# One interruption per query tile or chunk, earlier chunk loads, and all weight remainders on VectorE, in a hybrid attention and Mamba-2 block

## The chip, the cores and the metric

The kernel runs on one core of a Trainium2 chip. It is one decoder block on 512 tokens, in one launch. The metric is device time in microseconds (us). Five engines work side by side, each through its own instructions in their order, and wait for each other by semaphores: TensorE (PE in the profile, its weight loads PEld), VectorE (DVE), ScalarE (ACT), GpSimd (POOL), and SyncE (SP), which here issues all DMA transfers.

## The reference, cut to what matters

```python
h = rms_norm(x, norm_mix_g)                               # x: 512 tokens x 1024
q, k, v, z, xbc, dt_raw, gate_logits = split(h @ w_in)    # 1024 -> 10272 columns
# attention branch: 8 heads, two maps of 64 per head, values of 128
q = rms_norm(q) * scale; k = rms_norm(k)
for i in range(4):                                        # query tiles of 128
    logits = einsum('hmqd,hmkd->hmqk', q[tile i], k) + t5_bias, causal
    p = softmax(logits);  a = p[:, 0] - lam * p[:, 1]
    o[tile i] = a @ v
y_attn = rms_norm(o, attn_subln_g) * (1 - lam_init)
# Mamba-2 branch: 4 groups of 8 heads, state of 128
xbc = silu(causal_dwconv(xbc)); xs, bm, cm = split(xbc); dt = softplus(dt_raw + dt_bias)
for c in range(4):                                        # chunks of 128 tokens
    cum = cumsum(dt * a); decay = exp(cum[:, None] - cum[None, :]), causal
    y_diag = ((cc @ bc.T) * decay) @ xc
    y_off = (cc @ state) * exp(cum)
    state = state * exp(total) + (bc * w).T @ xc
y = rms_norm((y + xs * d_skip) * silu(z))                 # by group
mixed = sigmoid(g_attn) * (y_attn @ w_proj_attn) + sigmoid(g_ssm) * (y_ssm @ w_proj_ssm)
x = x + mixed @ w_out
u = causal_dwconv(rms_norm(x) @ w_up)
x = x + (silu(u_gate) * u_val) @ w_down                   # 2816 hidden columns
```

## The kernel before, in words

**Weights.** All weights stand in one stream `ws` of units of 128x1024 floats, in the order in which they are used (179 units, list `order` at the end of the file). `Weights.load` (L76) brings the next unit: a DMA writes `wr` (L80), ScalarE rounds it to the faster format as `wh` (L82), and a subtraction makes the remainder `wl` (L85). It runs on VectorE, but for units 71 to 90 on GpSimd (`pool_units`, L74 and L84). Every large product is three matmuls of 512 columns: `wh` by the rounded activations, `wh` by their remainder, `wl` by the rounded ones (L201 to L203 and like lines). Here these are called projections.

**The state-space stage.** 64 projection units (`SSD_UNITS`) run one after the other: B, C, x and z tiles of a group, the gate tiles e, and p, the products of a finished group with `w_proj_ssm`. After unit n the program adds what the dictionary `at` holds under n; these are the small steps, in full-precision matmuls that interrupt the projections. `SSD_AT` (L59) gives per group the units after which they stand. `chunk_pre` (L377) loads the decay rows of a chunk (`dec`), makes their exponentials on ScalarE, and the product of C and B (L388) times `dec` on VectorE (L391). `chunk_state` (L404) is the product with the state (L412, tile `yo`) and the new state (L419). `chunk_out` (L429) is the diagonal part (L435), which reads `dec`. `chunk_stat` (L445) sums squares, and `group_norm` (L459, L466 to L471) makes `yH` and `yL`, which the p units read. Tokens of x and B are turned by `flip` (L305, L308). The steps take their PSUM tiles from the pool `sm` (3 buffers).

**The attention stage.** `pieces` is a list of pieces of projections of about 6 to 12 matmuls: `pair_pieces` make q, k and v of two heads, `gate_pieces` a gate tile, `pa_pieces` three of the tiles of `w_proj_attn`. The dictionary `todo` holds what stands behind each piece. For a head, `prep` (L585) transposes q and k into two buffers (L591, pool `tpp`, 2 buffers), and ScalarE and VectorE read them (L599 to L607; `ql` is L601). Then come, for each of four query tiles, `logits` (L616), `flip_a` (L649, also from `tpp`) and `values` (L657); the last `values` of a head starts a chain over ScalarE, VectorE (`rsqrt`, L113) and GpSimd (L677), and `head_out` (L679, L682, again from `tpp`) needs its end. In the last pair the chain's end is what the rest of the kernel (from L756) waits for.

**What sets the order.** The program's order and the pools are given; a scheduler of the framework lays out the queues of the five engines from it, and may put an instruction a few places later or earlier where it reckons with a wait. Each engine then takes its queue strictly in order.

Of the kernel before, what the change touches and what calls it, by code (L numbers as in the profile page):

```python
# [9 lines left out]
F32 = mybir.dt.float32  # L10
# [8 lines left out]
P = 128  # L19
S = 512  # L20
D = 1024
NK = 8
NCH = 4
NG = 4
HPG = 8
NH = 8
# [18 lines left out]
def _units():  # L45
# [6 lines left out]
    for g in (2, 3):  # L52
# [3 lines left out]


SSD_UNITS = _units()
SSD_AT = [(11, (12, 14, 16, 18), (12, 15, 17, 19), 21, 23),  # L59
# [3 lines left out]


class Weights:


    def __init__(self, tc, ctx, ws, ahead):
        self.nc, self.tc, self.ws, self.ahead = tc.nc, tc, ws, ahead
        self.raw = ctx.enter_context(tc.tile_pool(name="wraw", bufs=3))  # L70
        self.parts = ctx.enter_context(tc.tile_pool(name="wparts", bufs=4))
        self.at = 0
        self.ready = []
        self.pool_units = frozenset(range(71, 91))  # L74

    def load(self, ahead=None):  # L76
        nc = self.nc
        with self.tc.high_priority(offset=ahead or self.ahead):
            raw = self.raw.tile([P, 1024], F32, name="wr")
            nc.sync.dma_start(out=raw, in_=self.ws[self.at])  # L80
            hi = self.parts.tile([P, 1024], F32R, name="wh")
            nc.scalar.copy(out=hi, in_=raw)  # L82
            lo = self.parts.tile([P, 1024], F32R, name="wl")
            eng = nc.gpsimd if self.at in self.pool_units else nc.vector  # L84
            eng.tensor_sub(out=lo, in0=raw, in1=hi.bitcast(F32))  # L85
        self.at += 1
        self.ready.append((hi, lo))

# [7 lines left out]
def block_kernel(ctx, tc, xt, ws, cols, heads, lams, relb, ident_d, ut_d, onehot_d, mline_d, out):  # L96
    nc = tc.nc
# [115 lines left out]
    cum_d = dram.tile([NG, NCH, HPG, P], F32, name="cum_d")  # L213
    ecum_d = dram.tile([32, S], F32, name="ecum_d")
# [75 lines left out]
    groups = [{} for _ in range(NG)]  # L290
# [20 lines left out]
    def tokens_b(st):  # L311
        tp = flip(st["B"])
        st["Bt"] = sp.tile([P, NCH, P], F32, name="Bt")
        A.copy(out=st["Bt"].rearrange("p c n -> p (c n)"), in_=tp)
# [10 lines left out]
    def unit(n, name, g):  # L325
        kind, j = name[0], int(name[1]) if len(name) > 1 else 0
        st = groups[g]
        if kind == "B":
            st["B"] = sp.tile([P, S], F32, name="Bc")
            conv_tile(16 + g, st["B"])  # L330
            at.setdefault(n + (2 if n else 4), []).append(lambda: tokens_b(st))
        elif kind == "C":
            st["C"] = sp.tile([P, S], F32, name="Cc")
            conv_tile(20 + g, st["C"])
        elif kind == "x":
            if j == 0:
                st["x"] = [sp.tile([P, S], F32, name="xtok", bufs=8) for _ in range(NCH)]
                st["Y"] = sp.tile([P, 4, S], F32, name="Y")
            xc = sp.tile([P, S], F32, name="xc", bufs=3)
            conv_tile(4 * g + j, xc)  # L340
            A.activation(out=st["Y"][:, j], in_=xc, func=AF.Copy, scale=pc[:, C_DK + 4 * g + j:C_DK + 4 * g + j + 1])
            at.setdefault(n + (3 if n < 4 else 2), []).append(lambda: tokens_x(g, j, xc))
        elif kind == "z":
            if j == 0:
                st["z"] = sp.tile([P, 4, S], F32, name="sz")
            ps = in_ctile()
            zs = st["z"][:, j]
            V.scalar_tensor_tensor(out=zs, in0=ps, scalar=0.5, in1=r_bc, op0=ALU.mult, op1=ALU.mult)
            zt = sp.tile([P, S], F32, name="raw")
            A.activation(out=zt, in_=zs, func=AF.Tanh)  # L350
            V.scalar_tensor_tensor(out=zs, in0=zt, scalar=1.0, in1=zs, op0=ALU.add, op1=ALU.mult)
        elif kind == "e":
            if j % 4 == 0:
                gates.append(sp.tile([P, 4, S], F32, name="Y" if j else "sz"))
            ps = in_ctile()
            gt = gates[-1][:, j % 4]
            V.tensor_mul(out=gt, in0=ps, in1=r_bc)
            A.activation(out=gt, in_=gt, func=AF.Tanh, scale=0.5)
        else:
            h, l = W.next()  # L360
            for i in range(2):
                c = 2 * j + i
                ps = ctile(lambda k: (h[:, (i * 4 + k) * P:(i * 4 + k + 1) * P], l[:, (i * 4 + k) * P:(i * 4 + k + 1) * P]),
                           4, lambda k: st["yH"][:, k, :], lambda k: st["yL"][:, k, :])
                if g == 0:
                    A.copy(out=acc[c], in_=ps)
                else:
                    V.tensor_add(out=acc[c], in0=acc[c], in1=ps)
                if g == NG - 1:
                    V.scalar_tensor_tensor(out=acc[c], in0=gates[c // 4][:, c % 4], scalar=1.0, in1=acc[c],  # L370
                                           op0=ALU.add, op1=ALU.mult)
# [2 lines left out]
    h3 = lambda t: t.rearrange("p (h d) -> p h d", h=HPG)  # L374
    j4 = lambda t: t.rearrange("p (j l) -> p j l", j=4)

    def chunk_pre(g, c):  # L377

        st = groups[g]
        cs = slice(c * P, (c + 1) * P)  # L380
        dec = sp.tile([P, HPG, P], F32, name="dec", bufs=3)
        nc.sync.dma_start(out=dec, in_=cum_d[g, c].partition_broadcast(P))
        for h in range(HPG):
            A.activation(out=dec[:, h], in_=dec[:, h], func=AF.Relu, scale=-1.0,
                         bias=qcol[:, 0, c, g * HPG + h:g * HPG + h + 1])
        A.activation(out=dec, in_=dec, func=AF.Exp, scale=-1.0)
        pcb = sm.tile([P, S], F32, name="sm")[:, :P]
        T.matmul(pcb, lhsT=st["B"][:, cs], rhs=st["C"][:, cs], start=True, stop=True)  # L388
        cb = sp.tile([P, P], F32, name="cb")
        V.tensor_mul(out=cb, in0=pcb, in1=ut)  # L390
        V.tensor_mul(out=dec, in0=dec, in1=cb.unsqueeze(1).to_broadcast([P, HPG, P]))  # L391
        st["dec", c] = dec
        if c < NCH - 1:
            xw = st["xw", c] = sp.tile([P, S], F32, name="xw")
            G.tensor_mul(out=h3(xw), in0=h3(st["x"][c]),
                         in1=qcol[:, 1, c, g * HPG:(g + 1) * HPG].unsqueeze(2).to_broadcast([P, HPG, 64]))
        if c > 0:
            ec = st["ec", c] = sp.tile([P, 4, P], F32, name="ec")
            for m in range(2):
                nc.sync.dma_start(out=ec[m * 64:(m + 1) * 64], in_=bass.AP(  # L400
                    tensor=ecum_d.tensor, offset=ecum_d.offset + (g * HPG + m) * S + c * P,
                    ap=[[0, 64], [2 * S, 4], [1, P]]))

    def chunk_state(g, c):  # L404

# [64 lines left out]
            A.copy(out=st["yH"][:, j], in_=Y[:, j])  # L470
            V.tensor_sub(out=st["yL"][:, j], in0=Y[:, j], in1=st["yH"][:, j].bitcast(F32))  # L471

    for g, (first, states, outs, last, norm) in enumerate(SSD_AT):
        def put(n, f, *a):
            at.setdefault(n, []).append(lambda: f(*a))
        put(first, chunk_pre, g, 0)
        for c in range(NCH):
            put(states[c], chunk_state, g, c)
            if c > 0:
                put(outs[c], chunk_stat, g, c - 1)  # L480
            put(outs[c], chunk_out, g, c)
            if c + 1 < NCH:
                put(outs[c], chunk_pre, g, c + 1)
        put(last, chunk_stat, g, NCH - 1)
        put(norm, group_norm, g)

# [225 lines left out]
    for p_ in range(4):  # L712
        start.append(len(pieces))
        if p_ < 3:
            pieces += pair_pieces(p_ + 1) + gate_pieces(p_)
        else:
            for c in range(3, 8):
                pieces += gate_pieces(c)
            pa = [pa_pieces(c) for c in range(3)]
            pieces += [f for q in pa for f in q[:3]] + [q[3] for q in pa]  # L720
# [1 line left out]
    def put(n, f, *a):  # L722
        todo.setdefault(n, []).append(lambda: f(*a))

    put(start[0] - 3, prep, 0)
    for p_ in range(4):
        for e, (prep_at, ats) in enumerate(zip((5, 22), ((0, 3, 7, 10), (14, 17, 21, 24)) if p_ < 3 else ((0, 3, 6, 9), (12, 15, 18, 21)))):
            h = 2 * p_ + e
            if h < NH - 1:
                put(start[p_] + prep_at, prep, h + 1)  # L730
            for i, n in enumerate(ats):
                n += start[p_]
                lag = 7 if p_ < 3 else 6
                put(n, logits, h, i)
                put(n + lag, flip_a, h, i)
                put(n + lag + 2, values, h, i)
            put(ats[3] + start[p_] + lag + 7, head_out, h)
    for n, f in enumerate(pieces):
        f()
        for g in todo.pop(n, []):  # L740
# [188 lines left out]
```

## Time and profile before

| | |
|---|---|
| median of three runs | 1175.27 us (1171.23 to 1176.12) |
| the profiled execution | 1176.51 us |
| its span, first to last instruction | 1174.7 us |
| mean granted TensorE clock | 0.984 |
| busy: TensorE matmul, VectorE, ScalarE, GpSimd | 1130.8, 770.5, 579.2, 166.5 us |
| state-space units | about 48 to 410 us of the span |
| q, k, v of the first two heads | about 410 to 475 us |
| attention, heads among projections | about 475 to 737 us |
| w_proj_attn, w_out, and the gated MLP | from about 737 us |

The matmul spans overlap, since matmuls are pipelined, so a busy TensorE can still lose time: what counts is how far apart two starts lie, and the waits. A wait is shown with the instruction that ended it. A stretch's granted clock (PEclk) is 1.00 at 2.4 GHz and 0.50 at 1.2 GHz. Durations of VectorE instructions include time in which the engine stood still inside them.

### The profile page before, as it was taken

What the parts mean: (1) busy time and instruction counts of PE and PEld (TensorE: products, weight loads), DVE (VectorE), ACT (ScalarE), POOL (GpSimd) and SP (SyncE); (2) the same over time, 40 slices, a digit from 0 to 9 for tenths busy, and PEclk for the clock granted to TensorE, in tenths of its full rate; (3) what the DMA queues carried; (4) which work ended last, traced back from release to release, by engine and by line L of the source; (5) the groups of instructions that cost most, each with busy time, mean ns of one, the idle gap of its engine ahead of it and who ended that gap; (6) DMA issues with size and microseconds to landing.
All of it is one profiled execution on the core that took longest, in us unless ns stands there. A gap on an engine that the chain in (4) does not pass through costs nothing.

```text
span 1174.7 us, 15747 instructions
## 1 busy us (share of the span) xinstructions
PE 1130.8 (96%) x5934; PEld 956.2 (81%) x5934; DVE 770.5 (66%) x1259; ACT 579.2 (49%) x1122; POOL 166.5 (14%) x177
## 2 busy tenths in 40 slices
PE   7999998999999999998989997999999999999998
PEld 5788876887887889998888876887888888888887
DVE  7858777768786573576767874745777777772221
ACT  5785655765664233656556663334444444441120
POOL 1003212112132201432432100012000000000000
PEclk9999998999999999998989999999999999999999
DMA  7463332333432222221212120343233332333420
GB/s 243 114 125 112 112 110 88 112 116 114 125 112 95 83 90 85 74 76 59 78 59 69 62 73 18 109 160 108 90 92 106 90 102 95 93 105 108 120 96 18
DMA packets 56124, 114.46 MB, mean 97 GB/s; under 512 B 20640, under 2 KB 28496, under 8 KB 56048
## 3 DMA queue, kind: packets, MB, share of 16 engines
q1 hardware_dynamic: 56048, 113.45, 31.6%
q8 instruction: 47, 0.77, 0.3%
q14 instruction: 29, 0.24, 0.1%
HBM read 111.19 MB, written 2.24 MB: 97 GB/s over the span
## 4 chain that ended last, share of the span: by engine, by line
PE 87%; DVE 7%; ACT 3%; issue 2%; POOL 1%; DMA 0%; SPq 0%; ACTq 0%; POOLq 0%; DVEq 0%
PE mm L201 20%; PE mm L202 20%; PE mm L203 20%; PE mm L524 4%; PE mm L522 4%; PE mm L523 4%; PE po L663 1%; DVE wl L85 1%; PE sm L435 1%; PE mm L539 1%; PE mm L540 1%; PE mm L538 1%; PE mm L756 1%; PE mm L757 1%; PE mm L758 1%
## 5 line engine op out<-in xcount | busy, mean ns | idle before, releaser
L82 ACT CAST wh<-wr 128x1024 fp32r<-128x1024 f32 x179 | 187.4, 1048 | 229.8 <-PE mm L202 190.5
L85 DVE TENSOR_TENSOR wl<-wr,wh 128x1024 fp32r<-128x1024 f32 x159 | 196.7, 1238 | 106.7 <-ACT wh L82 105.1
L201 PE MATMUL mm<-xH,wh 128*128 128x512 f32 x392 | 159.2, 406 | 7.8 <-ACT xH L173 7.2
L202 PE MATMUL mm<-xL,wh 128*128 128x512 f32 x392 | 154.9, 395 | 0.0
L203 PE MATMUL mm<-xH,wl 128*128 128x512 f32 x392 | 154.7, 395 | 0.0
L201 PE MATMUL mm<-hH,wh 128*128 128x512 f32 x352 | 137.1, 390 | 0.0
L203 PE MATMUL mm<-hH,wl 128*128 128x512 f32 x352 | 137.0, 389 | 0.0
L202 PE MATMUL mm<-hL,wh 128*128 128x512 f32 x352 | 137.0, 389 | 0.0
L522 PE MATMUL mm<-wh,xH 128*128 128x256 f32 x384 | 111.3, 290 | 0.0
L524 PE MATMUL mm<-wh,xL 128*128 128x256 f32 x384 | 109.9, 286 | 0.0
L523 PE MATMUL mm<-wl,xH 128*128 128x256 f32 x384 | 109.7, 286 | 0.0
L201 PEld LDWEIGHTS mm<-xH,wh 128*128 128x128 f32 x392 | 74.6, 190 | 24.1 <-ACT xH L173 7.2
L202 PEld LDWEIGHTS mm<-xL,wh 128*128 128x128 f32 x392 | 74.6, 190 | 16.0 <-DVE xL L174 1.0
L203 PEld LDWEIGHTS mm<-xH,wl 128*128 128x128 f32 x392 | 74.4, 190 | 16.3 <-DVE wl L85 0.3
L202 PEld LDWEIGHTS mm<-hL,wh 128*128 128x128 f32 x352 | 66.1, 188 | 13.8
L201 PEld LDWEIGHTS mm<-hH,wh 128*128 128x128 f32 x352 | 66.1, 188 | 13.7
L203 PEld LDWEIGHTS mm<-hH,wl 128*128 128x128 f32 x352 | 66.1, 188 | 13.5
L523 PEld LDWEIGHTS mm<-wl,xH 128*128 128x128 f32 x384 | 74.4, 194 | 0.3
L524 PEld LDWEIGHTS mm<-wh,xL 128*128 128x128 f32 x384 | 74.4, 194 | 0.0
L522 PEld LDWEIGHTS mm<-wh,xH 128*128 128x128 f32 x384 | 74.2, 193 | 0.2
L201 PE MATMUL mm<-aH,wh 128*128 128x512 f32 x176 | 68.5, 389 | 0.0
L202 PE MATMUL mm<-aL,wh 128*128 128x512 f32 x176 | 68.5, 389 | 0.0
(240 smaller groups left out, 2264.9 us busy)
## 6 DMA issues: line engine op xcount, KB each, us to landing
wr<-in_ws SPq DMA_DIRECT2D x179, 512.0 KB, 3.5
dec<-cum_d SPq DMA_DIRECT2D x16, 512.0 KB, 5.2
ec<-ecum_d SPq DMA_DIRECT2D x24, 128.0 KB, 3.9
x<-in_xt SPq DMA_DIRECT2D x4, 512.0 KB, 4.7
xr<-in_xt SPq DMA_DIRECT2D x8, 256.0 KB, 2.6
out_y<-x SPq DMA_DIRECT2D x8, 256.0 KB, 2.0
b<-line_d SPq DMA_DIRECT2D x8, 128.0 KB, 2.8
pc<-in_cols SPq DMA_DIRECT2D x1, 173.5 KB, 3.7
```

The lines of the kernel that those rows point to most:

```text
L82: nc.scalar.copy(out=hi, in_=raw)
L85: eng.tensor_sub(out=lo, in0=raw, in1=hi.bitcast(F32))
L201: T.matmul(ps, lhsT=h, rhs=rH(k), start=(k == 0), stop=False)
L202: T.matmul(ps, lhsT=h, rhs=rL(k), start=False, stop=False)
L203: T.matmul(ps, lhsT=l, rhs=rH(k), start=False, stop=(k == n - 1))
L435: T.matmul(yd[(h % 2) * 64:(h % 2) * 64 + 64, (h // 2) * P:(h // 2 + 1) * P], lhsT=xk[:, h * 64:(h + 1) * 64], rhs=dec[:, h], start=True, ...
L522: T.matmul(ps, lhsT=xH[k][:, sl], rhs=h, start=(k == 0), stop=False)
L523: T.matmul(ps, lhsT=xH[k][:, sl], rhs=l, start=False, stop=False)
L524: T.matmul(ps, lhsT=xL[k][:, sl], rhs=h, start=False, stop=(k == NK - 1))
L538: T.matmul(ps, lhsT=hk, rhs=xH[k], start=(k == 0), stop=False)
L539: T.matmul(ps, lhsT=hk, rhs=xL[k], start=False, stop=False)
L540: T.matmul(ps, lhsT=lk, rhs=xH[k], start=False, stop=(k == NK - 1))
```

## The change: what it does

Three things are changed. In the state-space stage a chunk has one place instead of two: the state part, the diagonal part, the preparation of the next chunk and the old chunk's sum all stand after one unit, with the token flips in front of them. The loads of `dec` and `ec` become a step of their own (`chunk_load`), two chunks ahead, and the first preparation of a group stands 3 or 4 units before its first chunk. The norm of group 0 stands after unit 22 instead of 23.

In the attention stage 37 steps are laid over the pieces. At step n stand the logits of query tile n, the flip of tile n-2 and the values of tile n-3. `prep` moves to 5 or 6 pieces before a head's first step, `head_out` to two steps behind the head's last values. Gate tile 2 moves from the third stretch of pieces to the last.

All remainders are subtracted on VectorE; `pool_units` goes.

```diff
-SSD_AT = [(11, (12, 14, 16, 18), (12, 15, 17, 19), 21, 23),
+SSD_AT = [(8, 10, (12, 14, 16, 19), 21, 22),
...
-        self.pool_units = frozenset(range(71, 91))
...
-            eng = nc.gpsimd if self.at in self.pool_units else nc.vector
-            eng.tensor_sub(out=lo, in0=raw, in1=hi.bitcast(F32))
+            nc.vector.tensor_sub(out=lo, in0=raw, in1=hi.bitcast(F32))
...
-            at.setdefault(n + (3 if n < 4 else 2), []).append(lambda: tokens_x(g, j, xc))
+            at.setdefault(n + (3 if n < 4 else 2), []).insert(0, lambda: tokens_x(g, j, xc))
...
+    def chunk_load(g, c):
+        st = groups[g]
+        dec = st["dec", c] = sp.tile([P, HPG, P], F32, name="dec", bufs=3)
+        nc.sync.dma_start(out=dec, in_=cum_d[g, c].partition_broadcast(P))
+        if c > 0:
+            ec = st["ec", c] = sp.tile([P, 4, P], F32, name="ec")
...
-    for g, (first, states, outs, last, norm) in enumerate(SSD_AT):
+    for g, (dec0, xw0, chunks, last, norm) in enumerate(SSD_AT):
         def put(n, f, *a):
             at.setdefault(n, []).append(lambda: f(*a))
-        put(first, chunk_pre, g, 0)
-        for c in range(NCH):
-            put(states[c], chunk_state, g, c)
+        put(dec0 - 1, chunk_load, g, 0)
+        put(dec0, chunk_pre, g, 0)
+        put(xw0, chunk_load, g, 1)
+        put(xw0, chunk_in, g, 0)
+        for c, n in enumerate(chunks):
             if c > 0:
-                put(outs[c], chunk_stat, g, c - 1)
-            put(outs[c], chunk_out, g, c)
+                put(n, chunk_stat, g, c - 1)
+            put(n, chunk_state, g, c)
+            put(n, chunk_out, g, c)
+            if c + 2 < NCH:
+                put(n, chunk_load, g, c + 2)
             if c + 1 < NCH:
-                put(outs[c], chunk_pre, g, c + 1)
+                put(n, chunk_pre, g, c + 1)
+                put(n, chunk_in, g, c + 1)
...
-    put(start[0] - 3, prep, 0)
+    steps = []
     for p_ in range(4):
-        for e, (prep_at, ats) in enumerate(zip((5, 22), ((0, 3, 7, 10), (14, 17, 21, 24)) if p_ < 3 else ((0, 3, 6, 9), (12, 15, 18, 21)))):
...
+        steps += [start[p_] + n for n in ((0, 3, 7, 10, 14, 17, 21, 24) if p_ < 2 else range(0, 24, 3))]
+    steps += [steps[-1] + n for n in (3, 6, 9, 12, 15)]
+    for h in range(NH):
+        first = steps[4 * h] if h else start[0] + 1
+        put(first - 6 if h % 2 else first - 5, prep, h)
+    for n in range(4 * NH + 5):
+        for f, back in ((logits, 0), (flip_a, 2), (values, 3)):
+            if 0 <= n - back < 4 * NH:
+                put(steps[n], f, (n - back) // 4, (n - back) % 4)
+        if n >= 8 and n % 4 == 0:
+            put(steps[n], head_out, n // 4 - 2)
```

Three places in the queues show it. In the changed file a line stands 2 lines higher up to L375, and up to 11 lines lower behind that. The first is TensorE's queue where group 0 is normed (`tp<-t,ones`) and the first chunk of group 1 runs. Before:

```order
L466 MATMUL tp<-t_1496,ones 128x128 x4
L419 MATMUL sm<-xw,Bt 128x512
L435 MATMUL sm<-dec,xtok 64x128 x8
L388 MATMUL sm<-Cc,Bc 128x128
L412 MATMUL sm<-Cc,state 128x128 x4
L201 MATMUL mm<-yH,wh 128x512 x2
```

The same place in the changed kernel:

```order
L306 MATMUL mm<-ident,Bc 128x128 x4
L471 MATMUL tp<-t_1519,ones 128x128 x2
L424 MATMUL sm<-xw,Bt 128x512
L471 MATMUL tp<-t_1519,ones 128x128 x2
L440 MATMUL sm<-dec,xtok 64x128 x8
L396 MATMUL sm<-Cc,Bc 128x128
L199 MATMUL mm<-xH_87,wh 128x512
```

Before, the product that reads `yH` follows at once, with the second chunk's state part (L412) pulled ahead of it; now a z tile of 24 projections stands in between, and the second chunk's part comes after the p and x units.

The second is VectorE's queue around the `prep` of head 2, whose `ql` frees a transpose buffer. Before:

```order
L643 RECIPROCAL es<-sums 128x2
L645 SCALAR_TENSOR_TENSOR cf<-es,nlam,sums 128x1
L646 SCALAR_TENSOR_TENSOR p<-p,cf 128x384
L601 TENSOR_TENSOR ql_3907<-tp,qq_4962 64x512
L633 TENSOR_TENSOR lg<-lg,bias 128x256
L601 TENSOR_TENSOR ql_3908<-tp,qq_4966 64x512
```

The same place in the changed kernel:

```order
L657 SCALAR_TENSOR_TENSOR p<-p,cf 128x384
L83 TENSOR_TENSOR wl<-wr,wh 128x1024 x2
L644 TENSOR_TENSOR lg<-lg,bias 128x256
L684 TENSOR_SCALAR ov<-ov 128x4
L644 TENSOR_TENSOR lg<-lg,bias 128x256
L115 TENSOR_SCALAR rsi<-ov 128x4
L612 TENSOR_TENSOR ql_3907<-tp,qq_4975 64x512
L116 TENSOR_SCALAR rsy<-rsi 128x4
L618 SCALAR_TENSOR_TENSOR ks_4983<-tp,gqk,ks_4983 64x512
L118 SCALAR_TENSOR_TENSOR rst<-rsy 128x4
```

Two subtractions that stood on GpSimd now stand ahead of `ql`, and `ql` stands among the small instructions of the head's `rsqrt`.

The third is TensorE's queue at the end of the last head. Before:

```order
L663 MATMUL po<-vt,aT 128x128 x4
L701 MATMUL mm<-yaH_3883,wh 128x512
L702 MATMUL mm<-yaL_3891,wh 128x512
L703 MATMUL mm<-yaH_3883,wl 128x512
...
L682 MATMUL tp<-ident,o 128x128 x4
```

The same place in the changed kernel:

```order
L674 MATMUL po<-vt,aT 128x128 x4
L712 MATMUL mm<-yaH_3879,wh 128x512
L713 MATMUL mm<-yaL_3887,wh 128x512
...
L714 MATMUL mm<-yaH_3883,wl 128x512
L693 MATMUL tp<-ident,o 128x128 x4
```

Between the last values and the last `head_out` stood 6 projections, and now stand 21.

## Rows read from the trace of the kernel before

**Rows 1.** The page: busy us, share of the span, instructions of each engine.
```profile
PE 1130.8 (96%) x5934; PEld 956.2 (81%) x5934; DVE 770.5 (66%) x1259; ACT 579.2 (49%) x1122; POOL 166.5 (14%) x177
```

**Rows 2.** Waits of TensorE, whole span: us in total, times, longest.
```profile
PE tp L682 <- DVE ql L601: 8.2, 3, 3.6
PE tp L682 <- POOL o L677: 6.7, 3, 5.3
PE tp L653 <- DVE ql L601: 6.3, 4, 2.8
PE sm L412 <- ACT state L422: 3.1, 1, 3.1
PE tp L591 <- POOL qk L570: 1.8, 2, 1.2
PE sm L435 <- DVE dec L391: 1.4, 1, 1.4
PE mm L201 <- ACT yH L470: 1.2, 1, 1.2
```

**Rows 3.** Stretches: length, busy us (instructions) by engine, PEclk, DMA share, GB/s.
```profile
177.40:187.70 10.30, 7.26 (x20) 5.89 (x21) 10.30 (x15) 5.14 (x11) 3.95 (x5) 0.50 0.31 102
532.40:539.30 6.90, 5.88 (x17) 4.83 (x18) 4.67 (x7) 3.82 (x9) 0.94 (x2) 0.51 0.46 147
563.10:566.60 3.50, 3.50 (x16) 3.31 (x15) 2.93 (x15) 2.03 (x7) 0.63 (x1) 0.51 0.35 140
730.40:737.30 6.90, 4.62 (x12) 3.44 (x13) 2.18 (x5) 2.50 (x3) 1.04 (x1) 0.51 0.01 2
```

**Rows 4.** Timeline, TensorE, one interruption by a flip: start, us, instruction.
```profile
72.61 0.39 PE L203 MATMUL mm<-xH,wl 128*128 128x512 f32 x1
72.84 0.60 PE L308 MATMUL mm<-ident,xc 128*128 128x128 f32 x4
73.19 0.48 PE L201 MATMUL mm<-xH,wh 128*128 128x512 f32 x1
73.50 0.40 PE L202 MATMUL mm<-xL,wh 128*128 128x512 f32 x1
```

**Rows 5.** Timeline around 528 us: GpSimd, VectorE, TensorE.
```profile
527.94 5.01 POOL L85 TENSOR_TENSOR wl<-wr,wh 128x1024 fp32r<-128x1024 f32 x2
528.10 2.65 DVE L646 SCALAR_TENSOR_TENSOR p<-p,cf 128x384 f32<-128x384 f32 x1
533.42 1.09 PE L682 MATMUL tp<-ident,o 128*128 128x128 f32 x4 [3.61 <-DVE ql L601]
```

**Rows 6.** Groups, GpSimd, 410 to 737: count, busy us, mean ns, idle before.
```profile
L85 POOL TENSOR_TENSOR wl<-wr,wh 128x1024 fp32r<-128x1024 f32 x20 | 48.1, 2421 | 78.7 <-ACT wh L82 78.6
```

**Rows 7.** Groups, VectorE, 470 to 656.
```profile
L646 DVE SCALAR_TENSOR_TENSOR p<-p,cf 128x128 f32<-128x128 f32 (+3 forms) x22 | 26.0, 1180 | 0.7
```

**Rows 8.** Groups, VectorE, 656 to 737.
```profile
L85 DVE TENSOR_TENSOR wl<-wr,wh 128x1024 fp32r<-128x1024 f32 x8 | 10.5, 1314 | 0.6 <-ACT wh L82 0.6
L646 DVE SCALAR_TENSOR_TENSOR p<-p,cf 128x384 f32<-128x384 f32 (+3 forms) x10 | 5.8, 576 | 0.2
```

**Rows 9.** Stretches of the attention stage, columns as in rows 3.
```profile
526.00:592.00 66.00, 59.60 (x435) 57.01 (x434) 47.07 (x111) 40.13 (x103) 23.51 (x13) 0.92 0.20 61
656.00:705.00 49.00, 46.61 (x254) 38.71 (x253) 37.81 (x80) 32.64 (x79) 2.48 (x3) 1.00 0.24 76
```

**Rows 10.** Waits of TensorE, 656 to 737.
```profile
PE tp L682 <- DVE ql L601: 1.0, 1, 1.0
PE tp L653 <- DVE ql L601: 0.5, 1, 0.5
```

**Rows 11.** Timeline at the last head's end.
```profile
724.16 1.05 PE L663 MATMUL po<-vt,aT 128*128 128x128 f32 x8
730.82 1.04 POOL L677 TENSOR_TENSOR o<-o,orr 128x512 f32<-128x512 f32 x1 [17.40 <-DVE orr L676]
731.91 1.12 PE L682 MATMUL tp<-ident,o 128*128 128x128 f32 x4 [5.32 <-POOL o L677]
```

More of the change, by code (lines that the diff above doesn't have):

```diff
@@ L330, in unit @@
             conv_tile(16 + g, st["B"])
-            at.setdefault(n + (2 if n else 4), []).append(lambda: tokens_b(st))
+            at.setdefault(n + (2 if n else 4), []).insert(0, lambda: tokens_b(st))
         elif kind == "C":
@@ L375, in block_kernel @@
     j4 = lambda t: t.rearrange("p (j l) -> p j l", j=4)
+    def chunk_load(g, c):
[4 more added lines that the diff above has]
+            ec = st["ec", c] = sp.tile([P, 4, P], F32, name="ec")
+            for m in range(2):
+                nc.sync.dma_start(out=ec[m * 64:(m + 1) * 64], in_=bass.AP(
+                    tensor=ecum_d.tensor, offset=ecum_d.offset + (g * HPG + m) * S + c * P,
+                    ap=[[0, 64], [2 * S, 4], [1, P]]))
     def chunk_pre(g, c):
@@ L380, in chunk_pre @@
         cs = slice(c * P, (c + 1) * P)
-        dec = sp.tile([P, HPG, P], F32, name="dec", bufs=3)
-        nc.sync.dma_start(out=dec, in_=cum_d[g, c].partition_broadcast(P))
+        dec = st["dec", c]
         for h in range(HPG):
@@ L391, in chunk_pre, with chunk_in @@
         V.tensor_mul(out=dec, in0=dec, in1=cb.unsqueeze(1).to_broadcast([P, HPG, P]))
-        st["dec", c] = dec
+    def chunk_in(g, c):
+        st = groups[g]
         if c < NCH - 1:
@@ L396, in chunk_pre @@
                          in1=qcol[:, 1, c, g * HPG:(g + 1) * HPG].unsqueeze(2).to_broadcast([P, HPG, 64]))
[L397 to L402, printed above, removed]
     def chunk_state(g, c):
@@ L714, in block_kernel @@
         if p_ < 3:
-            pieces += pair_pieces(p_ + 1) + gate_pieces(p_)
+            pieces += pair_pieces(p_ + 1) + (gate_pieces(p_) if p_ < 2 else [])
         else:
-            for c in range(3, 8):
+            for c in range(2, 8):
                 pieces += gate_pieces(c)
@@ L723, in put @@
         todo.setdefault(n, []).append(lambda: f(*a))
-    put(start[0] - 3, prep, 0)
+    steps = []
     for p_ in range(4):
-        for e, (prep_at, ats) in enumerate(zip((5, 22), ((0, 3, 7, 10), (14, 17, 21, 24)) if p_ < 3 else ((0, 3, 6, 9), (12, 15, 18, 21)))):
[L728 to L737, printed above, removed]
+        steps += [start[p_] + n for n in ((0, 3, 7, 10, 14, 17, 21, 24) if p_ < 2 else range(0, 24, 3))]
[9 more added lines that the diff above has]
+            put(steps[n], head_out, n // 4 - 2)
     for n, f in enumerate(pieces):
@@ L887 @@
         order += [q_[2 * p_:2 * p_ + 2], k_[2 * p_:2 * p_ + 2], v_[2 * p_:2 * p_ + 2]]
-        if p_ > 0:
+        if 0 < p_ < 3:
             order.append(gate[p_ - 1:p_])
-    order += [gate[3:8], pa]
+    order += [gate[2:8], pa]
     order.append(wo)
```

6 rows, old and new, of the table SSD_AT are left out of this document.

## The prediction, made before the change ran

> **What bounds the kernel now.** I read the page first: TensorE is busy for 96% of the span [rows 1], so a change helps only where TensorE waits, or where its clock is low. So the second view is TensorE's own waits [rows 2]: those listed make 28.7 us, in few places. Of these, 14.5 are waits of a transpose for `ql` (8.2 and 6.3), that is for a `tpp` buffer which `prep` still holds; 6.7 are waits of `head_out` for the end of its chain on GpSimd; and 5.7 lie together in the state-space stage, where group 0 is normed. The third view is the granted clock by stretch [rows 3]: behind the wait of 3.6 us at 533 it reads 0.51 (the level of 1.2 GHz) for 6.9 us, behind one of 2.8 for 3.5 us, behind the last `head_out`'s for 6.9 us, and behind the norm's for 10.3 us. The 3.6 and the 2.8 occur twice, at 597 and at 628 again, so there are six such stretches. What they cost is half of TensorE's busy time in them, since the work would take half as long at 2.4 GHz: 3.6 (norm), 2.9 and 1.8 (each twice), 2.3 (end), 15.3 together. Waits and clock are some 44 of 1174.7 us, and most that this change can give.
>
> The change is named for shared interruptions, so their price comes next [rows 4]. A projection follows the one before in 0.23 us (72.61 to 72.84). Four transposes take 0.35 us from the first's start to the next projection's, and that one's successor comes after 0.31 us, 0.08 late; but the fourth transpose, begun just before the projection, has 0.1 us of work of its own, so the switch itself is worth some 0.02 us.
>
> Why is `ql` late? At 528 VectorE's 128x384 instruction takes 2.65 us, while GpSimd does two remainders [rows 5]; the same line has a mean of 1180 ns while GpSimd makes remainders, and 576 later, where VectorE makes them [rows 7, 8]. VectorE stands still inside the instruction until GpSimd's ends, and `ql` is queued behind it.
>
> **State-space stage.** Waits removed: 3.1 (L412 for the state), 1.4 (L435 for `dec`), 1.2 (L201 for `yH`) [rows 2]. In the changed order `dec` of group 1 is made three units before its use instead of one; the state's next part stands two p and x units further on; and the p unit that reads `yH` and `yL` has a z tile of 24 projections (24 by 0.23, 5.5 us) in front. With the clock: 5.7 + 3.6 = 9.3 us. New: in those 5.5 us and the 2 to 2.5 that the group's own matmuls take, VectorE must do four norm multiplications, four `yL`, four steps of the C tile and a remainder. Twelve by an estimated 0.7 us (L646 takes 0.58 for a mean below 384 elements, these have 512) and 1.3 [rows 8] make 9.7, about 2 more than there is, so I keep 2.0 (bounds 0, since parts of it can start before, and 4, with one block as in rows 5). Gain 7.3. The loads themselves gain nothing: no wait of TensorE for a DMA is in the list. SyncE's queue is passed in nearly the same order.
>
> A chunk's step now takes four tiles of the three buffers of `sm`, so the C by B product (L396) waits until VectorE has read `yo`. By the queue it stands some 4 us behind the unit's end (a flip, 0.45 [rows 4], three products and two projections), and VectorE has three shorter instructions and a remainder to do until then: 3 by 0.58 and 1.3 [rows 8], 3.1 us, or 5.1 with a block of 2 [rows 5]. Bounds 0 and 1.1 for each of 11 steps; I take 0, since most of VectorE's instructions meet no block.
>
> **Attention, pairs 0 to 2.** GpSimd loses 20 subtractions of 2421 ns [rows 6], VectorE gains 20 of 1314, as it takes them later in the stage [rows 8]: 26.3 us. Against it, L646 alone loses (1180 - 576) by 22, 13.3 us, of standing still [rows 7, 8]; other lines lose some too. Net at most +13.0 us over three pairs, 4.3 each. A pair's 66 us hold 47.1 of VectorE [rows 9], and without the waits and the low clock below (half of 22.4) a pair is 54.8 long: VectorE then works 51.4 of 54.8, 94% at most. It does not bind, but it will be late at times. The waits for `ql` in these pairs are 8.2 - 1.0 and 6.3 - 0.5 [rows 2, 10], 13.0, the clock behind them 2 by 4.7, 9.4: together 22.4. What stays I read from the last pair, where VectorE already makes the remainders, GpSimd is nearly idle, and VectorE is at 77% [rows 9]: there TensorE waits 1.0 and 0.5 for `ql` [rows 10] and 1.4 for `head_out`'s chain (6.7 less 5.3) [rows 2, 11], 2.9 for two heads, with the clock at 1.00. Three pairs: 8.7. Gain 13.7. The bounds: nothing stays (22.4), or all does (0).
>
> The Trainium skill (SBUF — State Buffer, section Who interferes with whom) says that a VectorE instruction with two SBUF inputs and a GpSimd instruction that reads SBUF exclude each other, and whichever comes first holds the other up whole. The 2.65 us agree. By it a remainder on VectorE can also hold up the chain's GpSimd step; in the last pair, where that could happen, the waits above contain it, so the sum stays.
>
> **First prep.** It waits 1.8 us for GpSimd's scaling of q and k [rows 2]. That chain loses a block by a remainder, but `prep` moves up by a piece. I take 0 (bounds -1.5 and +1.5).
>
> **The end.** The last values start at 724.16; GpSimd's step ends at 731.86 and `head_out` starts at 731.91 after a wait of 5.3 us [rows 11]. Now 21 instead of 6 projections stand between: 15 by 0.23, 3.4 us more cover, all taken from earlier places where nothing waits for them. A wait of 1.9 stays. The clock's 2.3 goes if so short a wait leaves it up; the trace has none of this length, so I count half. Gain 4.6.
>
> **Interruptions.** 31 fewer on TensorE's queue, by 0.02: 0.6.
>
> **Sum.** 7.3 + 13.7 + 4.6 + 0.6 = 26.2 from the profiled execution's 1176.5: 1150.3. That execution lies 1.2 over the median, so 1149.
>
> **Rivals.**
> *All waits go.* If VectorE, freed from GpSimd, is never late, the 2.0, the 8.7 and the end's 1.9 and 1.2 go as well, and 2.9 in the last pair: 16.7 more, 1132. For it: `prep` and `flip_a` stand 3 to 5 us of projections apart in the new queue. Against: 94% on VectorE, and remainders ahead of `ql`. Chance 0.15.
> *The waits for `ql` keep their size.* VectorE gets back in remainders what it no longer loses. Then 13.7 falls away: 1163. For it: two remainders stand right ahead of `ql` in the prep of head 2. Against: the last pair, as above. Chance 0.17.
> *The chunk's step waits for its fourth PSUM tile.* 11 by 1.1 taken from the gain: 1161. For it: three buffers for four tiles, and 12 groups of them. Against: the 4 us above. Chance 0.10.
> *Slower: VectorE binds TensorE in pairs 0 to 2.* Place: the `ql` of six preps; price: two more remainders ahead of each, 2.6 us, and behind each wait the shortest low clock, 1.8: 26.4, while the old 22.4 stay and the other gains (12.5) come: 13.9 slower, 1189. It decides from the point where `ql` ends later than the flip behind a prep stands, 6 to 7 us after its transposes (by the queue, about three pieces' projections and a logits step); the instructions ahead of the second `ql` in its queue, an estimated 7 of 0.7 and two remainders by 1.3 [rows 8], take 7.5 if all stand there still. For it: this is close. Against: the block of 2 us at that place goes. Chance 0.05.
> *It does only what its name says.* Interruptions are saved, 0.6, and new waits replace the old: 1175. For it: every stall here is one of order, and orders can stall elsewhere. Against: the extra cover at the norm and at the end can be counted in the queue. Chance 0.05.
> My forecast: 0.48.
>
> **How the numbers follow.** About 0.5% (5.9 us) is what a measurement of this kernel can tell from no change. Faster by more: the forecast, the first three rivals, less the parts of the second and third that reach within 6 us of the old time: 0.87. Within 0.5%: 0.07. Slower: 0.06. The forecast's own range is 1142 to 1158: 7 us either way, for the bounds at the norm (2), the first prep (1.5), the end (1.2) and a third of what I let stay in the pairs, or as much again. The range reaches down to 1133, almost all of the first rival, and up to 1167, past the second and third and half way to no gain; beyond it lie the last two rivals and the tips of the first and second, some 0.2.
>
> **What would show each step.** In TensorE's waits of the changed kernel: no wait for the state, `dec` or `yH` around 160 to 185, at most about 2 us for `yL` in the p unit; if L396 waits for VectorE, the third rival holds. Waits for `ql` in pairs 0 to 2 of 1 to 1.5 us each and none of 2.8 or more; the 128x384 and like instructions of L657 near 0.6 us; VectorE's busy time per pair near 50 us. The last `head_out` waiting about 2 us instead of 5.3. Granted clock at 1.00 from 50 us on, with at most one low stretch at the end. The forecast is wrong if the low stretches in the attention stage stay, or if VectorE has hardly any idle time there.

## The result, and the profile after

The changed kernel takes 1159.41 us (median of 4 runs, 1156.54 to 1162.87), the kernel before 1175.07 beside it: ratio 0.9874, 95% interval 0.9837 to 0.9911, 15.7 us faster. Forecast were 1149 and 26.2 less. The direction and the wide range (1133 to 1167) held; the forecast's own range (1142 to 1158) was missed by 1.4 us, and ten microseconds of the forecast did not come. The profiled execution took 1162.87 us (span 1160.8, against 1174.7), and is the slowest of the four.

First TensorE's waits over the whole span, in the columns of [rows 2]:

```profile
PE tp L693 <- POOL o L688: 9.0, 7, 1.9
PE tp L602 <- POOL qk L581: 2.7, 3, 1.2
PE tp L471 <- ACT t L462: 2.5, 1, 2.5
PE mm L199 <- ACT acc L364: 1.7, 1, 1.7
PE tp L664 <- DVE ql L612: 1.6, 5, 0.5
PE sm L396 <- DVE t L420: 1.4, 2, 1.1
PE mm L200 <- DVE yL L476: 1.3, 2, 1.1
```

The 14.5 us for `ql` have become 1.6, and of the old waits in the state-space stage (state 3.1, `dec` 1.4, `yH` 1.2) none is left. But four new ones stand in that stage, for `t`, `acc`, `t` of the chunk's step, and `yL`: 2.5 + 1.7 + 1.4 + 1.3 = 6.9 us. The kernel before had 7.0 there: the 5.7 of [rows 2], 0.6 for `yL` and 0.7 for a flip.

Next VectorE from 470 to 656, columns as in [rows 7]; the remainders are L83 here, the combination of the two softmaxes L657:

```profile
L83 DVE TENSOR_TENSOR wl<-wr,wh 128x1024 fp32r<-128x1024 f32 x24 | 29.3, 1222 | 8.2 <-ACT wh L81 7.9
L657 DVE SCALAR_TENSOR_TENSOR p<-p,cf 128x128 f32<-128x128 f32 (+3 forms) x25 | 13.6, 542 | 0.5
```

L657 has fallen from 1180 to 542 ns, and a remainder costs 1222. Now stretches, columns as in [rows 3]. The first two lines hold nearly the same work (429 and 430 matmuls), from the first q product of pair 2 to that of pair 3 (counted from 0), before and after; the other two are the changed kernel's low clock:

```profile
540.51:605.69 65.18, 58.78 (x429) 56.16 (x428) 46.61 (x107) 39.57 (x100) 23.51 (x13) 0.92 0.20 62
534.23:590.99 56.76, 54.95 (x430) 52.84 (x429) 42.45 (x115) 39.80 (x101) 6.84 (x6) 1.00 0.23 70
715.90:722.70 6.80, 6.02 (x16) 4.60 (x17) 2.98 (x4) 3.51 (x4) 0.00 (x0) 0.50 0.00 0
797.80:801.20 3.40, 3.40 (x11) 2.82 (x11) 2.70 (x17) 0.00 (x0) 0.00 (x0) 0.50 0.09 35
```

The pair takes 8.4 us less, and VectorE is busy for 4.2 us less in it, though it now makes the remainders. Of the half-clock stretches before the last 20 us, six before, two remain: one at the end of the attention stage, and a new one behind the 1.2 us that the sums of squares behind the mix wait for GpSimd.

Last the end of the last head, as in [rows 11]:

```profile
708.12 1.05 PE L674 MATMUL po<-vt,aT 128*128 128x128 f32 x8
714.78 1.04 POOL L688 TENSOR_TENSOR o<-o,orr 128x512 f32<-128x512 f32 x1 [15.44 <-DVE orr L687]
715.88 1.11 PE L693 MATMUL tp<-ident,o 128*128 128x128 f32 x4 [1.93 <-POOL o L688]
```

5.32 has become 1.93, as worked out (1.9). The clock fell behind it all the same.

To add this up I read four starts of the same instruction in both traces: the first projection (before 7.22, after 8.78), the first attention projection (444.16, 444.82), the first product behind the last head (733.80, 717.76), the first of the MLP (808.30, 792.98). The second of them shows that the state-space units, with their last p products, run to 444 us before, not to 410 as the table ahead of the prediction has it, and that q, k and v start there. The state-space stage went from 436.9 to 436.0 us, the attention stage from 289.6 to 272.95, the mix from 74.5 to 75.2, the MLP from 366.4 to 367.8. So the attention stage gave 16.7 us, the state-space stage 0.9, and the rest took 3.7 back (the start 1.6; the mix and the MLP 2.1, which I put down to the half clock there). That is the 13.9 us between the two traced executions, not the 15.7 between the medians.

### The profile page after: what moved, and what is told of

Its sections match the earlier page's. It is cut to its first block, busy times and chain, and to the rows that moved or that the text cites. A ratio compares the mean times of both kernels' runs of the same rounds, so it can differ in the third digit from the quotient of the medians.

```text
span 1160.8 us, 15739 instructions
## 1 busy us (share of the span) xinstructions
PE 1123.5 (97%) x5934; PEld 945.8 (81%) x5934; DVE 764.0 (66%) x1279; ACT 578.9 (50%) x1122; POOL 125.1 (11%) x157
## 5 line engine op out<-in xcount | busy, mean ns | idle before, releaser
L83 DVE TENSOR_TENSOR wl<-wr,wh 128x1024 fp32r<-128x1024 f32 x179 | 219.4, 1227 | 114.9 <-ACT wh L81 113.0
```

The source lines that it names most:

```text
L83: nc.vector.tensor_sub(out=lo, in0=raw, in1=hi.bitcast(F32))
```

## The experiments

Two theories stood against each other. **Lock**: the time came from the 20 remainders that left GpSimd, since a GpSimd subtraction stops VectorE while it runs; the state-space stage gave nothing, because new waits and more switching on TensorE ate what the old waits returned. **Order**: the time came from the new places of the steps, and the remainders are only work that changed hands. All runs were timed beside the kernel before (medians 1173.8 to 1174.4 us).

### The parts of the change, each alone

```
e1  before + SSD_AT and the chunk functions of the change
e2  before:  -  eng = nc.gpsimd if self.at in self.pool_units else nc.vector
             +  eng = nc.vector
e3  before + steps, prep, head_out, gate_pieces of the change
e4  e2 and e3 together
```

Expected of e1: 

> The kernel before with only the state-space stage's new order and loads. Theory (cost theory): what the new order saves in waits at 160 to 200 us it pays back in new waits and in switching around the 64-wide tiles, as the two traces show (excess of the stage 20.5 us before, 19.9 after): 0 to 2 us faster, about 1174, the waits for state, dec and yH gone, a wait of L471 for t of about 2.5 us there. Rival (the prediction's own term): the stage gives 7.3 us, 1168, and the changed kernel's stage only looks bad beside the other two parts.

Of e2: 

> The kernel before with only its 20 remainders of units 71 to 90 moved from GpSimd to VectorE. Lock theory: the standing still of VectorE inside L646 and its neighbours goes (about 29 us over the stage, 3.5 in the changed kernel), the waits for ql shrink to 1 to 1.5 us each and the four half-clock stretches at 530 to 635 go: 10 to 14 us faster, about 1163. Order theory (rival): what made ql late is the old places of prep and of the transposes; VectorE gets back in remainders what it no longer loses, so the waits stay: within 3 us of before, 1173 to 1176.

Of e3: 

> The kernel before with only the attention stage's new order (steps, prep, head_out, one more gate tile at the end); the 20 remainders stay on GpSimd. Lock theory: the end of the stage gives its 3.6 us and the spared interruptions 0.4 to 0.6, the blocks inside VectorE stay and some half-clock stretches between 500 and 660 with them: 3 to 6 us faster, 1170. Order theory: 12 to 16 us faster, 1160.

Of e4: 

> The changed kernel with the state-space stage as before. Cost theory: the stage's change is worth 0 to 2 us, so this is 1159 to 1162, the changed kernel's time. Rival (the prediction's term for the stage): 1166.

| | us | ratio to before, interval | attention stage, us |
|---|---|---|---|
| e1 state-space alone | 1173.81 | 1.0003 [0.9989, 1.0018] | 286.0 |
| e2 remainders alone | 1162.84 | 0.9906 [0.9888, 0.9924] | 274.1 |
| e3 attention's order alone | 1173.12 | 0.9995 [0.9984, 1.0006] | 286.1 |
| e4 remainders and order | 1160.59 | 0.9892 [0.9870, 0.9915] | 272.45 |

The one line of e2 is worth 10.9 us, most of the whole change. The new state-space stage is worth nothing that can be measured, and neither is the new attention order alone (I had expected 3 to 6). On top of the remainders the attention order adds 2.3 us (e4), and the state-space stage 1.2 more; neither is clear of the intervals. In e1 the waits for the state and `dec` are gone and that for `yH` is down to 0.2, and 2.3 for `t`, 1.4 at L396's place and 1.1 for `yL` stand there instead, as in the whole change. Waits of TensorE in e2, whole span:

```profile
PE tp L680 <- POOL o L675: 8.8, 5, 5.3
PE tp L680 <- DVE ql L599: 2.8, 3, 1.0
PE tp L651 <- DVE ql L599: 1.8, 4, 0.6
PE tp L589 <- POOL qk L568: 0.5, 1, 0.5
```

And in e3, where GpSimd still makes the remainders:

```profile
PE tp L682 <- POOL o L677: 13.1, 7, 3.3
PE tp L653 <- DVE ql L601: 5.0, 5, 1.6
PE tp L591 <- POOL qk L570: 4.4, 3, 2.1
```

In e2 the places of `prep` and of the transposes are the old ones, and the waits for `ql` still fall from 14.5 to 4.6: order alone did not make `ql` late. In e3 they fall to 5.0 too, but the blocks inside VectorE only meet another reader: `head_out` now waits 13.1 us instead of 6.7, `prep` 4.4 instead of 1.8, and half-clock stretches stand at 478, 543, 608 and 731. The waits for `ql`, `o` and the scaled q and k together are 23.0 us before, 22.5 in e3, 13.9 in e2 and 13.3 in the whole change. Of the half-clock stretches in the attention stage e2 keeps one of five, the one at its end (716). The attention stages of e1 and of the kernel before have the same code and differ by 3.6 us in these two executions, so a single trace does not settle a few microseconds; the medians do.

### GpSimd busy beside VectorE

```
   nc.vector.tensor_sub(out=lo, in0=raw, in1=hi.bitcast(F32))
+  if 71 <= self.at < 91:
+      nc.gpsimd.tensor_sub(out=raw, in0=raw, in1=hi.bitcast(F32))
```

Expected: 

> The changed kernel, and beside each of the 20 remainders of units 71 to 90 on VectorE a subtraction of the same shape on GpSimd, whose result (over the raw weights) nothing reads. Lock theory: a GpSimd instruction of 2.4 us stops VectorE whoever needs it, so L646 and its neighbours (here L657 too) get durations of 2 us and more again, some 20 us of standing still come on top of the remainders that VectorE now makes itself, waits for ql of 2 to 4 us and half-clock stretches return between 470 and 660: 15 us slower or more than the changed kernel, 1174 to 1190. Rival (the remainders were slow on GpSimd, and what waited, waited for wl or its queue): nothing waits for the added instructions, 1158 to 1161.

It takes 1179.65 us, 1.0047 of the kernel before [1.0030, 1.0065], 20 us over the changed kernel, though nothing reads what GpSimd makes. Two of TensorE's waits, whole span:

```profile
PE tp L666 <- DVE ql L614: 10.3, 5, 3.4
PE tp L604 <- POOL qk L583: 6.3, 3, 4.5
```

And one block in the timeline of GpSimd (its added subtraction is L85) and VectorE:

```profile
469.87 2.41 POOL L85 TENSOR_TENSOR wr<-wr,wh 128x1024 f32<-128x1024 f32 x1 [1.16 <-DVE wl L83]
470.16 2.16 DVE L575 TENSOR_SCALAR qkv<-qkss 128x32 f32<-128x32 f32 x1
475.06 3.76 POOL L583 TENSOR_TENSOR qk<-qk,qkr 128x1024 f32<-128x1024 f32 x2 [2.79 <-DVE qkr L580]
```

An instruction on 32 columns takes 2.16 us and ends with GpSimd's, at 472.3. Behind it TensorE waits 4.5 us for the scaled q and k, and the clock falls at 476.8. GpSimd's own queue did not make that scaling (L583) late: GpSimd had been idle for 2.79 us, until VectorE's factors came. Some fifteen of VectorE's instructions between 470 and 700 stand still under such a subtraction, 23 us by their excess over the shortest of their kind. Where I said which, I was wrong: the softmax combination keeps its 536 ns; those hit are the remainders and the small steps of the norms. The Trainium skill (SBUF — State Buffer, section Who interferes with whom) counts a tensor_scalar among those that can take both of VectorE's port pairs and so contend with GpSimd; this one, with a single input, agrees. The held raw buffer is no other cause: for `wl` TensorE waits 0.4 us in all.

### What stayed: three edits on the changed kernel

```
e6  -  if n >= 8 and n % 4 == 0:   put(steps[n], head_out, n // 4 - 2)
    +  if n >= 9 and n % 4 == 1:   put(steps[n], head_out, n // 4 - 2)
    +  (the last head's stays; pa's third pieces behind all first and second)
e7  -  (8, 10, (12, 14, 16, 19), 21, 22)
    +  (8, 10, (12, 14, 16, 18), 20, 22)   and all chunk_stat of a group at `last`
e8  -  steps[-1] + n for n in (3, 6, 9, 12, 15)
    +  steps[-1] + n for n in (3, 5, 7, 9, 15)
```

Expected of e6: 

> The changed kernel with head_out of heads 0 to 6 one step (about three pieces) later, and the third pieces of the last gate products behind all first and second ones, since they need head 6. The waits of L693 for o (9.0 us, 7 of them, 1.0 to 1.9 each) are late by less than one step's 4 us: heads 0 to 5 wait no more, the last keeps its 1.9: 5 to 8 us faster, 1153. Rival: the tpp buffers are the limit, so the waits pass over to the transposes (L664, L602) behind: within 2 us, 1158 to 1161.

Of e7: 

> The changed kernel; group 0's last chunk and its sum one unit earlier (18 and 20 instead of 19 and 21), and the four 128x1 sums of squares of every group (L454) together at its last unit. Cost theory: L471's wait for t (2.5 us) goes, and 12 sums that stood alone (112 ns to the next matmul) cost 26 each: 1.0; together 3.5 us faster than the changed kernel, 1156, if no new wait comes at 170 to 200. Rival: the wait only moves to yL or acc, 2 us later in the same group: within 1.5 us, 1158 to 1161.

Of e8: 

> The changed kernel with the last head's last transposes one piece and its last values two pieces earlier (12 projections more behind them, 2.7 us). The last head_out's wait of 1.9 goes and with it the half clock behind it, if so short a wait brings it: 2 to 5 us faster, 1155. Rival: the softmax chain is late instead (a wait of the earlier transposes), or the clock falls behind the mix's wait of 0.8 all the same: within 1.5 us, 1158 to 1161.

| | us | ratio to before, interval | less than the changed kernel's 1159.4 |
|---|---|---|---|
| e6 head_out later | 1151.02 | 0.9807 [0.9789, 0.9825] | 8.4 |
| e7 sum earlier | 1155.46 | 0.9841 [0.9824, 0.9857] | 3.9 |
| e8 values earlier | 1156.27 | 0.9848 [0.9833, 0.9862] | 3.1 |

The last two gains are small beside the 7 us over which the changed kernel's own executions spread; but its ten (with the repetition e9 below) all took 1156.5 us or more, and the four of e7 and the four of e8 all 1156.8 or less.

e6's waits from 470 to 720: six of the seven for `o` are gone, and `prep` and the transposes wait as before, so the `tpp` buffers were not the limit. The 8.4 us are more than these 7.1: the low clock at the stage's end is also shorter in the traced execution, 3.4 us instead of 6.8.

```profile
PE tp L602 <- POOL qk L581: 2.9, 3, 1.2
PE tp L693 <- POOL o L688: 1.9, 1, 1.9
PE tp L664 <- DVE ql L612: 1.6, 5, 0.5
```

In e7 the wait for `t` (2.5) is gone. The second half of my reason is not borne out: a sum of squares that stands alone holds the next start back by 0.14 us, and the four together at the group's end take 0.81, so that edit gave nothing and by these starts lost 0.26 a group. What the wait was is seen in the changed kernel's timeline:

```profile
167.92 0.60 PE L306 MATMUL mm<-ident,Bc 128*128 128x128 f32 x4
171.00 0.78 PE L471 MATMUL tp<-t,ones 128*128 128x128 f32 x4 [2.48 <-ACT t L462]
```

L471 spreads the norm's factors. Group 0 was normed two units behind its sum before, and is normed one unit behind it in the change: the chain of small VectorE steps between was not over.

In e8 no `head_out` is waited for at the end, and no stretch of half clock follows there, though one stands behind the wait for `t` and one near 792.

### Once more, and all three

```
e9   the changed kernel, unaltered
e10  e6, e8 and the first line of e7
e11  e10, and  -  (19, 20, (22, 25, 29, 32), 34, 36)
               +  (19, 20, (22, 25, 28, 31), 33, 35)
```

Expected of e9: 

> The changed kernel itself once more, on the same chip as the two runs beside it: 1159, and by the cost theory the same waits (L471 2.5, acc 1.7, o 9.0) within 0.2 us; if the half-clock stretch at 798 is chance and not of this order, it is missing here (rival: it is there again).

Of e10: 

> The changed kernel with the edits of three runs that have each been faster: head_out one step later, the last head's values two pieces earlier, group 0's sum one unit earlier (the sums of squares stay where the changed kernel has them). Gains add where the waits are different ones: 8.4 (head_out) and 3.9 (sum) and about 3 (end, of which nothing is in the first), so 1144 (1142 to 1148). The sums of squares cost 112 ns each at the end of the group as well, so leaving them costs nothing. Rival: the engines that were late stay late and part of it comes back elsewhere: 1150.

Of e11: 

> The three edits, and group 1's third and last chunk, sum and norm one unit earlier too (28, 31, 33, 35 instead of 29, 32, 34, 36). The wait for yL at 275 (1.3 in the list, 1.9 by the pitches) goes, since the norm then has a z tile before its reader: 1.5 to 2 us faster than the run beside it. Rival: VectorE is behind there by more than one unit, and the wait moves to L396 or acc: within 0.5 us of it.

e9 takes 1161.14 us (1156.92 to 1163.26), 0.9884 [0.9866, 0.9903]. Its waits are the old ones within 0.2 us but for two that are missing, the 1.7 for `acc`, which I had expected again, and 1.0 for `wl`. Its clock is another. The stretch behind the same last `head_out` reads 1.00, there is none at 798, and a new one stands behind the wait for `t`:

```profile
170.70:174.10 3.40, 3.40 (x16) 2.16 (x16) 2.86 (x3) 2.60 (x6) 1.76 (x2) 0.50 0.17 14
715.40:722.20 6.80, 6.80 (x29) 5.25 (x30) 5.97 (x8) 2.95 (x3) 0.00 (x0) 1.00 0.25 69
```

So behind a wait of about 2 us the clock falls in some executions and not in others. The state-space stage took 435.4 us here, with the low clock and without the wait for `acc`, and 436.0 with that wait and without the low clock. The stretch near 798 is there in four of the eight kernels traced with the new state-space stage and in none of the four with the old; since the unaltered kernel lacks it the second time, it does not belong to the order alone, and whether the order makes it likelier stays open.

e10 takes 1144.44 us (1142.94 to 1144.82), 0.9742 [0.9726, 0.9758]: 15 us under the changed kernel, which the three gains add up to. Two of its stretches:

```profile
526.00:592.00 66.00, 65.12 (x509) 62.53 (x508) 50.95 (x140) 46.61 (x118) 7.69 (x7) 1.00 0.26 75
592.00:656.00 64.00, 62.23 (x450) 57.71 (x449) 51.01 (x128) 46.36 (x115) 7.25 (x6) 1.00 0.19 60
```

And the page's line on the engines, as in [rows 1]:

```profile
PE 1117.1 (98%) x5934; PEld 942.6 (83%) x5934; DVE 760.0 (67%) x1279; ACT 578.3 (51%) x1122; POOL 123.0 (11%) x157
```

No half clock stands between the start and the last microseconds, and its runs lie within 2 us of one another, those of the changed kernel within 7. e11 takes 1142.95, 0.9736 [0.9719, 0.9753], which cannot be told from e10: the wait for `yL` went, but L396's grew from 1.2 to 2.9 us. Its traced execution (1145.23) has one low stretch, 3.4 us at 473 behind two waits of `prep`, 1.7 us together, that e10 has too.

## Why the prediction was right, and where it was too large

By the number alone the result lies nearer to the third rival (1161) and the second (1163) than to the forecast (1149). The waits tell them apart: for `ql` TensorE waits 1.6 us where the second kept 14.5, for L396 1.4 where the third had 12.

**Pairs 0 to 2 of the attention stage, 13.7.** Right in cause and nearly in size. By TensorE's elapsed time less its instructions at their steady spacing, the loss between 470 and 705 fell by 12.4 us. e2 and e5 show the cause from both sides. One term was wrong in sign: the sum had VectorE 4.3 us a pair busier (51.4 of 54.8), and it is 4.2 less busy (42.45 of 56.76, before 46.61). I had counted the standing still in L646 alone; what VectorE got back in all is more than the remainders cost, and it did not bind. What stays is of another kind than I read from the last pair: for `ql` TensorE waits 1.6 us in all, for `head_out`'s chain 7.1 besides the end. With the old places (e2) that chain cost 3.5 besides the end and `ql` 4.6, so the new order moved this loss more than it took it away. It hung on `head_out`'s place: e6 took it by moving that call and the pieces that read its result.

**The end, 4.6.** The wait went as computed. The clock's half term is a matter of chance: it came in e9, where the clock stays up there, and not in the profiled execution, which by the same measure gained 3.6 us at the end.

**First prep, 0.** 1.8 became 2.7, inside the bounds.

**The state-space stage, 7.3.** This step failed. e1 puts it at nothing, within 0.2% either way. I listed what the new order takes away (5.7 of waits, which did go) and kept 2.0 for `yL`, the only new wait that I had looked for at the norm. `yL` has 1.3, but three others came in the profiled execution:

- `t`, 2.5: the norm moved to one unit behind the sum. I had counted the distance from norm to reader (24 projections more) and not the one from sum to norm, which paid for it. In e7, with the sum one unit earlier, the wait is gone.
- `acc`, 1.7. In GpSimd's timeline at that place:

```profile
181.47 3.41 POOL L443 TENSOR_TENSOR Y<-Y,sz 128x512 f32<-128x512 f32 x1 [5.67 <-DVE Y L442]
```

And in ScalarE's:

```profile
184.91 0.63 ACT L445 ACTIVATE t<-Y 128x512 f32<-128x512 f32 x1 [2.65 <-POOL raw L294]
187.42 0.57 ACT L364 COPY acc<-mm 128x512 f32<-128x512 f32 x1
```

L443 takes 1.29 us in ten of its 16 executions, 3.41 here, while VectorE runs two `yL` and a remainder from 181.3 to 183.7. (The L294 that the second view names is the memset of 0.10 us that follows L443 on GpSimd.) The norm now meets a chunk's step, and by these rows the same lock works the other way: GpSimd stands still, ScalarE waits for it with the copy out of PSUM queued behind, and TensorE has no free buffer. No edit was made to test this, but the nine traces with the new stage agree: in five L443 takes 3.0 to 3.4 us at this place and the wait for `acc` is 1.6 to 1.7; in the other four (e1, e5, e8, e9) it takes 1.3 to 1.7 and there is no such wait. In those four the clock had fallen behind the wait for `t`, and TensorE ran later. That the lock works both ways I had written for the attention stage, not here.
- L396, 1.4 in two of the steps, 1.1 the longest: the third rival, which had 11 by 1.1. It was right in kind, at about a tenth of the price.

And the steps that share an interruption do not switch less. One chunk's interruption in TensorE's timeline of the kernel before:

```profile
222.51 0.28 PE L449 MATMUL tp<-ones,sq 128*128 128x1 f32 x2
222.71 1.09 PE L435 MATMUL sm<-dec,xtok 128*64 128x128 f32 x16
223.74 0.49 PE L388 MATMUL sm<-Cc,Bc 128*128 128x128 f32 x2
224.06 0.60 PE L308 MATMUL mm<-ident,xc 128*128 128x128 f32 x4
224.42 0.48 PE L201 MATMUL mm<-xH,wh 128*128 128x512 f32 x1
```

And of the changed one, from the matmuls for the state on:

```profile
219.94 1.14 PE L417 MATMUL sm<-Cc,state 128*128 128x128 f32 x8
220.91 1.02 PE L424 MATMUL sm<-xw,Bt 128*128 128x512 f32 x2
221.87 1.09 PE L440 MATMUL sm<-dec,xtok 128*64 128x128 f32 x16
222.89 0.50 PE L199 MATMUL mm<-xH,wh 128*128 128x512 f32 x1
223.23 0.39 PE L200 MATMUL mm<-xL,wh 128*128 128x512 f32 x1
223.46 0.38 PE L396 MATMUL sm<-Cc,Bc 128*128 128x128 f32 x2
```

Two L424 take 0.96 us from 220.91 to the next start, though they follow each other after 0.43: the 64-wide L440 starts 0.52 after the second. Its last instruction keeps the next waiting 0.20, where a transpose lets a projection start after 0.03. These two changes stood in the old order as well, once a chunk, and L396, which used to stand behind the 64-wide ones, is now an interruption of its own. From its first start to the sixth projection behind, less the steady spacing of each instruction, the switching of a chunk costs about 0.44 us before and 0.55 or more after, some 2 to 3 us for 16 chunks, where I had put no cost. The stage's own balance agrees: the waits are level (7.0 and 6.9), the clock gave 3.6 back, and only 0.9 was gained, so 2.8 us went elsewhere. The Trainium skill (TensorEngine Tiling (Array Packing), section Key Properties) says that a change of tiling mode drains TensorE; the 0.52 against 0.43 agrees. That this cost and the new waits ate the whole of the old waits and of the norm's half clock is argued from the traces; e7, which takes the wait for `t` back and gains 3.9 us, is the run that shows a part of it.

**Interruptions, 0.6.** Spared were those of the attention stage (87 before, 57 after); the state-space stage has 46 before and 45 after, so one place for a chunk did not make them fewer. No run shows the 0.6 us by itself.

The sum took the clock's low stretches (15.3 us in six places) for fixed, but for the one at the end. They are not: executions of one kernel differ by up to 7 us, and the profiled one of the changed kernel had two stretches that its repetition had not, while the repetition had one of its own.

## What to carry to other kernels

Ask of an instruction on GpSimd not how long it takes but whom it stops: one line that took 20 remainders off it was worth 11 us, and the same work put back beside VectorE, for nothing, cost 20. When an order is rearranged to lengthen one distance (norm to reader), write down every distance in that chain, since the unit gained was taken from the next one (sum to norm). And look in the new profile for the same small wait repeated at the same place: six waits of 1.2 us on average went by moving one call and what reads its result. Once the waits of 2 us were gone too, the traced execution of e10 had no low clock on the way; that of e11 still had one stretch.

## What the runs showed of the hardware

A GpSimd subtraction of 128x1024 held a VectorE instruction of 32 columns, with one tensor input, for 2.16 us; a GpSimd multiplication of 128x512 took 3.41 us instead of 1.29 while VectorE ran subtractions with two tensor inputs. Behind the same wait (1.9 us, 2.5 us) the clock read 0.50 in one execution and 1.00 in another of the same kernel. Entering 64-wide matmuls cost 0.09 us and leaving them 0.20 to the next start. A 128x1 float32 matmul alone held the next start back by 0.14 us; four in a row took 0.81.
